# Input projection in seven-product form on x cast by DMA, residual added by DMA, MLP weights cast and summed in every group

## The chip, the cores and the metric

The kernel runs on all 8 cores of one Trainium2 chip. Each core works on its own 4096 tokens, and no core waits for another. The metric is device time in microseconds (us) of the slowest core, and less is better. Two kernels are compared on the same chip, in alternating rounds.

Each execution has a state. In the slow state the cores of one die, sometimes of both, show a lower granted TensorE clock than usual, and the execution takes some per cent longer. A ratio is the mean time of one kernel's fast runs over the mean time of the other kernel's fast runs of the same rounds, so it isn't quite the ratio of the medians that are quoted beside it.

PE is TensorE's matrix unit, PEld its weight loads, DVE VectorE, ACT ScalarE, POOL GpSimd and SP SyncE. The DMA share is the mean busy share of the core's 16 DMA engines.

## The reference

One block of a streaming encoder, width 1024, float32 in and out:

```python
h = rmsnorm(x, norm1_g)
b_gate, c_gate, xc, u, v = split(h @ w_in)        # 1024 -> 5 x 512
y_a = b_gate * causal_conv3(c_gate * xc, conv_w)
y_b = u * spatial_gating(layernorm(v), gmlp_ws, gmlp_bs)
y = concat(rmsnorm(y_a), rmsnorm(y_b))
x = x + y @ w_out                                 # the residual of this study
h2 = rmsnorm(x, norm2_g)
a = relu(h2 @ w_up)                               # 1024 -> 4096
x = x + (a * a) @ w_down
return rmsnorm(x, final_g)
```

## The kernel before

A core first runs the mixing stage over 8 tiles of 512 tokens, from about 20 to 400 us. Its result `x1` goes to HBM. Then the MLP runs over 4 groups of 1024 tokens; each group has two halves, and each half an up and a down projection. The 32 MLP weight blocks pass through a ring of six buffers, once per group, so 128 loads in all.

The output projection and the MLP are computed in a seven-product form: operands are split in 2x2 blocks, and seven block products replace eight. The price is sums: on each side the seven blocks come from four by four additions or subtractions, and the products are then added up. For the weights, `wsum` does the first part:

```python
def wsum(p, n):                       # three DVE instructions
    tt(p[:, 4], p[:, 3], p[:, 2], ALU.add, ...)
    tt(p[:, 3:6:2], p[:, 0:1] (twice), p[:, 3:5], ALU.subtract, ...)
    tt(p[:, 6], p[:, 1], p[:, 5], ALU.add, ...)
```

Before, these sums are formed once. 24 of the 32 weights are prepared during mixing and 8 at first use, and all seven blocks are stored in HBM as float16 (0.9 MB). The groups then load finished sums:

```python
def combine(p, dst, src, ...):
    dma("pool", p[:, 0:4], src[i % 16], ...)          # float32 -> float16, 1 MB read
    wsum(p, 128)
    dma("sp", dst, p[:, :], ...)                      # seven blocks to HBM

def load_w(n):
    if n < 32 and i >= 24:
        combine(RING[s], ws(i), wdn_d, ...)
    else:
        dma("sp", RING[s][:, :, :, :], ws(i), ...)    # 0.9 MB of float16
```

The input projection is plain, in matmuls of 512 columns. The residual is added by DVE straight from PSUM into the tile of x that is in SBUF anyway:

```python
def add(h, d_, bank):                 # in out_proj
    v = x[:, d_:d_ + 2, half * h:half * (h + 1)]
    tt(v, bank[:, :], v, ALU.add, ...)
# [cut] then dma("sp", x1_d part, x part)
```

## Time and profile before

| | before |
|---|---|
| time, median of 3 runs | 1234.01 us (1233.76 to 1235.53) |
| PE busy | 1195.1 us, 97% of the span |
| DVE, ACT busy | 76%, 43% |
| chain that ended last | 88% PE, 8% DMA |

From the page of the slowest core come the busy times, the PE and DMA rows of 40 slices (a digit is tenths of the slice that the unit was busy) and the chain of waits by engine:

```profile
PE 1195.1 (97%) x6264; PEld 584.4 (47%) x6264; DVE 939.3 (76%) x1460; ACT 533.5 (43%) x905; POOL 82.0 (7%) x144
...
PE   5899999999999999999999999999999999999994
...
DMA  7977888696676869357898954667964655975424
...
PE 88%; DMA 8%; DVE 1%; issue 1%; ACT 1%; SPq 0%; DVEq 0%; ACTq 0%; POOLq 0%
```

PE is the limit: it is busy for 90% or more of every slice but the first two and the last.

The windows view cuts one core's span into stretches. Its columns are the stretch, its length, then the busy time of PE, PEld, DVE, ACT and POOL (with the number of instructions), the granted clock, the DMA share and GB/s.

The timeline of PE shows small statistics products in each mixing tile (start, duration, instruction). The starts of the first one of each tile give the length of a tile:

```profile
175.99 0.59 PE L506 MATMUL PS<-SQ_61,ONESE 128*128 128x512 bf16 x2
227.57 0.59 PE L506 MATMUL PS<-SQ_61,ONESE 128*128 128x512 bf16 x2
277.42 0.59 PE L506 MATMUL PS<-SQ_61,ONESE 128*128 128x512 bf16 x2
327.69 0.59 PE L506 MATMUL PS<-SQ_61,ONESE 128*128 128x512 bf16 x2
```

Tiles are 50 to 52 us apart.

### The profile page before, as it was taken

What the parts mean: (1) busy time and instruction counts of PE and PEld (TensorE: products, weight loads), DVE (VectorE), ACT (ScalarE), POOL (GpSimd) and SP (SyncE); (2) the same over time, 40 slices, a digit from 0 to 9 for tenths busy, and PEclk for the clock granted to TensorE, in tenths of its full rate; (3) what the DMA queues carried; (4) which work ended last, traced back from release to release, by engine and by line L of the source; (5) the groups of instructions that cost most, each with busy time, mean ns of one, the idle gap of its engine ahead of it and who ended that gap; (6) DMA issues with size and microseconds to landing.
All of it is one profiled execution on the core that took longest, in us unless ns stands there. A gap on an engine that the chain in (4) does not pass through costs nothing.

```text
span 1233.4 us, 19511 instructions; the slowest of 8 cores (1226.8 to 1233.4 us)
## 1 busy us (share of the span) xinstructions
PE 1195.1 (97%) x6264; PEld 584.4 (47%) x6264; DVE 939.3 (76%) x1460; ACT 533.5 (43%) x905; POOL 82.0 (7%) x144
## 2 busy tenths in 40 slices
PE   5899999999999999999999999999999999999994
PEld 3345645546556464444444444444444444444442
DVE  2799889898899997448879747868746877856745
ACT  4554664555644555045047116217305417504533
POOL 0101011010001100001100100000000000100000
PEclk8999999999999999999999999999999999999998
DMA  7977888696676869357898954667964655975424
GB/s 184 163 162 197 202 219 202 175 258 153 176 234 182 294 219 301 119 183 174 222 309 270 282 204 159 212 199 223 296 230 150 218 185 172 296 252 179 150 90 137
DMA packets 60084, 253.87 MB, mean 206 GB/s; under 512 B 6224, under 2 KB 8400, under 8 KB 59984
## 3 DMA queue, kind: packets, MB, share of 16 engines
q1 hardware_dynamic: 38800, 182.36, 43.7%
q0 software_dynamic: 21184, 70.26, 25.9%
q8 instruction: 52, 0.85, 0.3%
q14 instruction: 48, 0.39, 0.1%
HBM read 211.71 MB, written 65.01 MB: 224 GB/s over the span
## 4 chain that ended last, share of the span: by engine, by line
PE 88%; DMA 8%; DVE 1%; issue 1%; ACT 1%; SPq 0%; DVEq 0%; ACTq 0%; POOLq 0%
PE PS L506 88%; DMA XS_92<-x_s 2%; DMA oT<-RA 1%; DMA RA<-x_s 1%; DMA WCXB_51<-wcxb 1%; DMA WV<-wv 1%; DMA X_75<-xT 1%; DMA WCXB_53<-wcxb 1%; DMA WSB_107<-wst 1%; DMA X_76<-xT 0%; DVE RB L522 0%; DVE RA L522 0%; SPq L533 0%; DVE H_93 L525 0%; ACT DUMP_57 L513 0%
## 5 line engine op out<-in xcount | busy, mean ns | idle before, releaser
L522 DVE TENSOR_TENSOR RB<-PS,RB 128x512 f32<-128x512 f32 x128 | 88.2, 690 | 84.6 <-PE PS L506 82.3
L522 DVE TENSOR_TENSOR RA<-PS,RA 128x512 f32<-128x512 f32 x96 | 66.0, 689 | 58.4 <-PE PS L506 55.6
L506 PE MATMUL PS<-YN,WO 128*128 128x256 f16 x896 | 104.7, 273 | 1.0 <-DVE YN L522 0.8
L522 DVE TENSOR_TENSOR A_86<-A_86 128x512 bf16<-128x512 bf16 (+1 forms) x192 | 93.9, 506 | 12.8 <-ACT A_86 L513 8.3
L506 PEld LDWEIGHTS PS<-YN,WO 128*128 128x128 f16 x896 | 87.3, 98 | 20.6 <-issue 2.8
L513 ACT ACTIVATE SN_88<-PS 128x512 f32<-128x512 f32 x63 | 37.2, 594 | 109.2 <-PE PS L506 108.7
L506 PE MATMUL PS<-A_86,RING_80 128*128 128x512 bf16 x308 | 76.7, 379 | 2.4 <-DVE RB L522 2.4
L506 PE MATMUL PS<-A_86,RING_82 128*128 128x512 bf16 x308 | 77.2, 379 | 0.0
L506 PE MATMUL PS<-A_86,RING_83 128*128 128x512 bf16 x308 | 77.1, 379 | 0.0
L506 PE MATMUL PS<-A_86,RING_81 128*128 128x512 bf16 x308 | 76.3, 379 | 0.0
L506 PE MATMUL PS<-H_93,RING_80 128*128 128x512 f16 x308 | 75.4, 379 | 0.0
L506 PE MATMUL PS<-H_93,RING_84 128*128 128x512 f16 x308 | 75.1, 379 | 0.0
L506 PE MATMUL PS<-H_93,RING_81 128*128 128x512 f16 x308 | 74.5, 379 | 0.0
L506 PE MATMUL PS<-H_93,RING_85 128*128 128x512 f16 x308 | 74.0, 379 | 0.0
L506 PE MATMUL PS<-A_86,RING_84 128*128 128x512 bf16 x280 | 69.6, 379 | 0.0
L513 ACT ACTIVATE SN_89<-PS 128x512 f32<-128x512 f32 x63 | 37.3, 594 | 74.5 <-PE PS L506 71.7
L506 PE MATMUL PS<-A_86,RING_85 128*128 128x512 bf16 x280 | 69.1, 379 | 0.0
L513 ACT ACTIVATE SN_87<-PS 128x512 f32<-128x512 f32 x66 | 39.0, 594 | 68.1 <-PE PS L506 64.7
L506 PE MATMUL PS<-H_93,RING_82 128*128 128x512 f16 x280 | 68.3, 379 | 0.0
L506 PE MATMUL PS<-H_93,RING_83 128*128 128x512 f16 x280 | 67.9, 379 | 0.0
L513 ACT ACTIVATE SN_90<-PS 128x512 f32<-128x512 f32 x64 | 38.1, 596 | 61.6 <-PE PS L506 61.3
L522 DVE TENSOR_TENSOR SN_89<-PS,SN_89 128x512 f32<-128x512 f32 x63 | 43.2, 688 | 24.8 <-PE PS L506 23.5
(237 smaller groups left out, 2078.4 us busy)
## 6 DMA issues: line engine op xcount, KB each, us to landing
RING_80<-ws_s SPq DMA_DIRECT2D x20, 896.0 KB, 5.9
RING_81<-ws_s SPq DMA_DIRECT2D x20, 896.0 KB, 6.3
RING_83<-ws_s SPq DMA_DIRECT2D x20, 896.0 KB, 6.5
RING_82<-ws_s SPq DMA_DIRECT2D x20, 896.0 KB, 5.6
RING_84<-ws_s SPq DMA_DIRECT2D x20, 896.0 KB, 6.2
RING_85<-ws_s SPq DMA_DIRECT2D x20, 896.0 KB, 6.2
ws_s<-PREP_70 SPq DMA_DIRECT2D x12, 896.0 KB, 5.7
ws_s<-PREP_69 SPq DMA_DIRECT2D x12, 896.0 KB, 6.0
```

The lines of the kernel that those rows point to most:

```text
L506: ins = e.matmul(real(o_), lhsT=l, rhs=r, start=st, stop=sp, skip_group_check=True)
L513: S.add("act", lambda e: e.activation(out=out, in_=real(in_), func=func, **kw), reads=reads, writes=writes, occ=(n / 1.2 + 100 + 70 * aps) ...
L522: dve(lambda e: e.tensor_tensor(out=out, in0=real(in0), in1=in1, op=op), reads, writes, n, rate, in0)
```

## The change

The intent is less PE work: the input projection gets the seven-product form too, which takes 280 matmuls of 256 columns per tile instead of 160 of 512. To pay for its sums and to make room in SBUF, DVE is relieved elsewhere. x arrives as float16, cast by the DMA, and isn't normalised. The residual is added by an accumulating DMA. The MLP's input isn't normalised either; its scale is carried to the residual and cancels in the last norm. The stored weight sums are gone: all 128 ring loads now read float32, cast, and form the sums again. The diffs here and below are shortened, with some helpers written out.

```diff
 def load_w(n):
-    if n < 32 and i >= 24:
-        combine(RING[s], ws(i), wdn_d, ...)
-    else:
-        dma("sp", RING[s][:, :, :, :], ws(i), ...)
+    dma("pool", p[:, 0:4, :, :], wup_d or wdn_d [i % 16], ...)   # 1 MB of float32, cast
+    wsum(p, 128)
 ...
 def load_x(m, chain=None, n=2):
-    dma("sp", X[...], xT part)                        # float32
+    dma("pool", HR[m % 2][:, j:j + n], xq[m, :, j:j + n], after, ...)   # cast to float16
 ...
 def out_proj(m):
-    winograd(prod, add, dc)                           # DVE adds PSUM to x
-    dma("sp", x1_d part, x part)
+    unit(prod, copy, copy, ...)                       # products into OB (copies on ACT, adds on DVE)
+    dma("pool", OB part, xT part, accum_op=ALU.add)   # residual
+    dma("sp", x1_d part, OB part)
 ...
-def stage_conv(m, c): ...   def stage_su(m, c): ...   def prep(i, n): ...
+def stage_c(m): unit(tprod(m, WC), ...)              # and stage_x, stage_v, gated alike
+def wsum_pe(w): ...                                   # first weight sums by identity matmuls
+def h_sums(m): ...                                    # sums of x's blocks, on DVE
```

## The prediction

> **What bounds the kernel now.** TensorE. On the page, PE is busy 1195.1 of 1233.4 us (97%), DVE 76%, ACT 43%; the chain of waits that ended last is 88% PE. From 150 us to the last down matmul at about 1217 the windows show PE busy almost throughout; the rest is start-up (about 20 us idle before 100 us, cold clock, DMA share about 1.0) and a 16 us tail. Only less PE work or a better start can pay, and a new wait can take it back.
>
> **PE.** In the timeline a 512-column matmul repeats every 216 ns and a 256-column one (64 of the output projection in 6.99 us) every 109 ns. The input projection has 160 of the former per token tile; in seven-product form 280 of the latter: 34.6 -> 30.6 us. Tile 0 stays plain, so 7 x 4.0 = 28 us go. Back come 66 identity matmuls forming weight sums at the start (14 us, partly in start-up holes) and some more statistics products. Summing both instruction orders with these durations: 1187 -> 1176 us. Net gain 11 us, not 28.
>
> **DVE and ACT.** Priced with durations of the trace (PSUM add 0.69 us, fp16 sum 0.42 for 512 and 0.68 for 1024 elements, f32 1024 product 1.22), DVE rises from 935 to about 1004 us: 96 more weight-sum triples (about 130 us) and the residual's products, against adds replaced by ACT's PSUM-to-PSUM copies, residual adds moved to DMA and dropped normalisations. ACT rises from 519 to about 700. In the mixing stage DVE falls to about 85% of a tile, ACT rises from 56% to over 80%. In the MLP, per half phase of 48.2 us PE, DVE carried 22 to 47 us; now 34 to 49. The fullest is the first down half of each group, 45 to 49: no slack.
>
> **DMA.** MLP weights now come as 1 MB of f32, cast, 128 times, not 0.9 MB fp16. From start-up and the queue table I estimate 4 us of all 16 engines per cast MB, against 2.7 for the old load: the MLP's DMA share goes from about 63% to about 85%. [...]its casts all sit on POOL's queue (25.9% of the engines' time). New coupling: DVE forms the sums in order, so a late weight stops DVE, and PE behind it.
>
> **On the critical path.** All PE time: -11. Start-up about -2 (loads still DMA-bound, but no x normalisation ahead of PE). New waits +5 to +20, mostly in the first up and down halves of groups 1 to 3, where output, residual loads and weights meet, and a little in mixing, where ACT copies gate the second product.
>
> **Predicted: 1224 us, 1209 to 1247 (8 in 10). Faster by over 2%: 0.10; within 2%: 0.83; slower: 0.07.**
>
> **What would show it.** Right: PE busy about 1180; mixing tiles about 47 us apart instead of 50; DVE over 90% in the first down halves, with small PE waits on DVE; DMA share over 0.8 through the MLP. Wrong: 256-column matmuls slower than 109 ns; PE idle of 30 us or more in the MLP behind weight loads (then slower); start-up idle under 10 us and PE without waits (then about 1205).
>
> **What would make it wrong.** Cast loads slower under load than at the start, so that six ring slots don't hide them; accumulating DMAs holding up output buffers; or a first tile beginning far earlier than the 18 us I expect.

"Its casts" are those of the trace of before: its DMA view has them on POOL's queue, with plain loads beside them. The windows of before, core 0, show what the start-up figures mean: a granted clock of 0.52 from 20 to 25 us and 0.80 from 25 to 30 us ("cold clock"), and a DMA share of 0.86 to 1.03 between 5 and 80 us, but for 0.62 from 20 to 25.

## More of the kernel before

The order of the instructions on each engine isn't written by hand. The program searches for it with a model of the engines and random draws, so any edit reshuffles all engines.

Core 0 of before, in mixing and at the entry of the MLP:

```profile
100.00:370.00 270.00, 269.19 (x1661) 148.71 (x1659) 246.02 (x349) 148.03 (x246) 22.85 (x43) 1.00 0.77 206
370.00:510.00 140.00, 139.83 (x797) 73.98 (x796) 119.82 (x178) 65.63 (x110) 12.63 (x21) 1.00 0.74 232
```

The length minus the first busy time is PE's idle time. It is 0.2 us at the entry, though that stretch holds the last tile of mixing, the first weights, the MLP's first inputs and the residual loads. The last number but one of each row, the DMA share, says that the DMA engines had a quarter of their time left.

The DMA view of the entry (kind of transfer, KB, median us from issue to landing) has the loads of the residual of the down projection, `RA` and `RB`:

```profile
RB<-x_s POOLq DMA_DIRECT2D x4, 512.0 KB, 12.9
RA<-x_s POOLq DMA_DIRECT2D x4, 512.0 KB, 11.9
```

## The result

The changed kernel is correct, and slower: 1285.39 us median (1271.72 to 1293.72, 4 runs, one of them slow) against 1234.77 us. The ratio of the fast runs is 1.0375 (95% interval 1.031 to 1.0441).

The same lines after. The page is that of core 7, the slowest:

```profile
PE 1214.1 (96%) x7346; PEld 699.0 (55%) x7346; DVE 997.9 (79%) x1654; ACT 697.8 (55%) x1203; POOL 115.9 (9%) x198
...
PE   4999999999997999999999989999999999989994
...
PEclk7999999999998788889999999999999999999997
...
DMA  9931663763459799456676965776896747897434
...
PE 84%; DMA 10%; DVE 2%; issue 2%; ACT 1%; SPq 0%; DVEq 0%; POOL 0%; ACTq 0%; POOLq 0%
```

The PE clock row dips from the thirteenth slice on. On cores 6 and 7 the granted clock was 0.81 from about 400 to 568 us. The other six cores, two of the same die among them, didn't hold it: from 510 to 568 us the windows view shows 1.00 on each of them. What set it off isn't shown. So the argument below uses core 0. The ratio above does contain this slower clock: cores 6 and 7 idled less (core 7 for 55.9 us in all, core 0 for 76.9) and were busy for longer (1214.1 us against 1192.6), and came out as late; and in each of the three fast runs some cores show a mean clock of 0.957 to 0.967, where the profiled run of before has 0.990 or more on every core. So core 0 is the measure of the waits, and the ratio is somewhat more than the waits alone. Its windows and its statistics products after:

```profile
100.00:370.00 270.00, 267.75 (x2569) 233.37 (x2568) 225.12 (x310) 205.97 (x371) 25.67 (x33) 1.00 0.50 106
370.00:510.00 140.00, 112.61 (x715) 68.11 (x714) 100.09 (x160) 81.48 (x140) 15.44 (x23) 0.94 0.92 193
...
1090.00:1150.00 60.00, 49.96 (x211) 21.28 (x209) 39.57 (x66) 6.01 (x10) 4.23 (x8) 0.91 0.80 163
```

```profile
130.35 0.59 PE L518 MATMUL PS<-SQ,ONESE 128*128 128x512 bf16 x2
175.78 0.59 PE L518 MATMUL PS<-SQ,ONESE 128*128 128x512 bf16 x2
221.20 0.59 PE L518 MATMUL PS<-SQ,ONESE 128*128 128x512 bf16 x2
268.38 0.59 PE L518 MATMUL PS<-SQ,ONESE 128*128 128x512 bf16 x2
```

Mixing did what it was meant to do: the tiles are 45 to 47 us apart, and PE idles for 2.2 of 270 us. The loss is in the next stretch. At the entry of the MLP PE idles for 27.4 us (140.00 - 112.61), and the DMA share is 0.92. Between 1090 and 1150 us another 10 us are lost.

A ledger for core 0, from the windows of both kernels. Its span grew by 36.1 us, from 1233.4 to 1269.5:

| PE idle time in (us) | before | after |
|---|---|---|
| 0 to 100 | 19.5 | 19.1 |
| 100 to 370 (mixing) | 0.8 | 2.2 |
| 370 to 510 (entry of the MLP) | 0.2 | 27.4 |
| 510 to 1090 | 2.4 | 3.2 |
| 1090 to 1200 | 0.0 | 10.0 |
| 1200 to the end | 15.5 | 15.0 |
| PE busy, whole span | 1195.1 | 1192.6 |

Idle time explains 38.6 us. The busy time fell by only 2.5 us, though the work fell by more, because matmuls ran slowly after the long pauses: in the first 3 us after a pause of 10.6 us, from 499.4 us on, the windows view shows a granted clock of 0.50, and from 502.4 us on 0.98 or more; after a pause of 5.9 us, from 1142 us on, it shows 0.50 for 3 us and 0.57 for 3 more. Core 0's mean clock was 0.983, where before had 0.992.

What stops PE there? The waits view of PE, core 0, 370 to 510 us (waited for: us in total, times, longest):

```profile
PE PS L518 <- DVE SN L539: 11.0, 2, 10.6
PE PS L518 <- ACT SN L525: 4.9, 2, 3.2
PE PS L518 <- ACT OB L525: 4.7, 3, 3.3
PE PS L518 <- ACT T L525: 4.4, 1, 4.4
```

They name DVE and ACT, but DVE was busy for only 100 of 140 us. The chain of waits of the same core, 370 to 530 us (start, us, what), names what those engines had waited for; its short pieces are left out:

```profile
378.57 19.41 DMA OB<-xT
398.05 9.37 DMA x_s<-OB
...
411.95 8.01 DMA OB<-xT
420.02 10.63 DMA x_s<-OB
...
444.86 17.47 DMA RING<-wup
...
469.10 25.35 DMA RB<-x_s
```

First the accumulating residual, then the store that must follow it, which holds the buffer OB; then a weight; then the residual of the down projection, for which DVE stood still for 11.4 us, with PE behind it for 10.6 us. The DMA view of that stretch, after (queue: packets, MB, share of the 16 engines; then each kind of transfer, as above):

```profile
q0 software_dynamic: 3493, 12.67, 55.8%
q1 hardware_dynamic: 4788, 14.18, 35.9%
...
OB<-xT POOLq DMA_DIRECT2D x9, 512.0 KB, 12.6
RING<-wup POOLq DMA_DIRECT2D x8, 512.0 KB, 17.4
...
RING<-wdn POOLq DMA_DIRECT2D x6, 512.0 KB, 13.8
RA<-x_s SPq DMA_DIRECT2D x4, 512.0 KB, 24.8
RB<-x_s SPq DMA_DIRECT2D x4, 512.0 KB, 25.6
```

Before, the loads of RA and RB took 11.9 and 12.9 us there. After, the median of all 64 RING<-wup on the page (core 7) is 6.3 us, and here it is 17.4. (The sizes are those of the destination; a cast from float32 to float16 reads twice as much.)

The 10 us lost after 1090 us are a wait of the same kind, and not for a weight. PE waited for DVE, which waited for the residual RB; the load of RB was issued only when stores of the output, one after another, had freed its buffer. The waits view of PE from 510 to 1200 us, and two pieces of the chain of waits:

```profile
PE PS L518 <- DVE RB L539: 13.2, 5, 5.9
...
1108.11 14.48 DMA oT<-RB
...
1122.65 17.32 DMA RB<-x_s
```

The theory (A): at the entry, late mixing and early MLP overlap, and the change gave both more DMA work, casting weight loads and accumulating residuals. Together they fill the DMA engines, the loads take two to three times as long, and those on PE's path stop PE. Rivals: (B) accumulation in itself, because a store, a reload and a free buffer wait behind it; (C) DVE, which forms 96 more weight sums and falls behind; (D) the order that the search happened to find.

### The profile page after: what moved, and what is told of

The parts are those of the page before. It is cut to its first block, busy times and chain, and to the rows that moved or that the text cites. A ratio compares the mean times of both kernels' runs of the same rounds, so it can differ in the third digit from the quotient of the medians.

```text
span 1270.0 us, 22374 instructions; the slowest of 8 cores (1255.6 to 1270.0 us)
## 1 busy us (share of the span) xinstructions
PE 1214.1 (96%) x7346; PEld 699.0 (55%) x7346; DVE 997.9 (79%) x1654; ACT 697.8 (55%) x1203; POOL 115.9 (9%) x198
## 4 chain that ended last, share of the span: by engine, by line
PE 84%; DMA 10%; DVE 2%; issue 2%; ACT 1%; SPq 0%; DVEq 0%; POOL 0%; ACTq 0%; POOLq 0%
PE PS L518 84%; DMA oT<-RB 3%; DMA x_s<-OB 2%; DMA OB<-xT 2%; DMA oT<-RA 1%; DMA RA<-x_s 1%; DMA RB<-x_s 1%; DMA WIN<-win 1%; DMA HR<-xq 1%; DVE RB L539 0%; DVE RA L539 0%; ACT RSY L525 0%; DVE A L539 0%; DVE RING L539 0%; ACT FSQ L525 0%
## 5 line engine op out<-in xcount | busy, mean ns | idle before, releaser
L518 PE MATMUL PS<-A,RING 128*128 128x512 bf16 x1792 | 408.7, 387 | 7.8 <-DVE RB L539 7.8
L518 PE MATMUL PS<-H,RING 128*128 128x512 f16 x1792 | 410.2, 388 | 0.0
L518 PEld LDWEIGHTS PS<-A,RING 128*128 128x128 f16 x1792 | 177.7, 99 | 229.4 <-issue 46.4
L518 PEld LDWEIGHTS PS<-H,RING 128*128 128x128 f16 x1792 | 178.6, 100 | 220.3 <-issue 40.6
L525 ACT ACTIVATE SN<-PS 128x512 f32<-128x512 f32 x256 | 149.7, 593 | 107.2 <-PE PS L518 101.8
L539 DVE TENSOR_TENSOR RING<-RING 128x512 f16<-128x512 f16 (+1 forms) x384 | 190.9, 505 | 6.0 <-DVE RING L539 0.5
L518 PE MATMUL PS<-HR,WIN 128*128 128x256 f16 x928 | 116.1, 277 | 2.2 <-ACT T L525 1.4
L518 PE MATMUL PS<-HD,WIN 128*128 128x256 f16 x896 | 112.4, 274 | 4.9 <-ACT T L525 3.4
L518 PEld LDWEIGHTS PS<-HR,WIN 128*128 128x128 f16 x928 | 91.4, 99 | 16.8 <-issue 3.0
L539 DVE TENSOR_TENSOR A<-A 128x512 bf16<-128x512 bf16 (+1 forms) x192 | 93.4, 506 | 5.2 <-ACT A L525 3.4
```

Source lines behind the costliest of these rows:

```text
L518: ins = e.matmul(real(o_), lhsT=l, rhs=r, start=st, stop=sp, skip_group_check=True)
L525: S.add("act", lambda e: e.activation(out=real(out), in_=real(in_), func=func, **kw), reads=reads, writes=writes, occ=(n / 1.2 + 100 + 70 ...
L539: dve(lambda e: e.tensor_tensor(out=out, in0=real(in0), in1=in1, op=op), reads, writes, n, rate, in0)
```

## The experiments

The expectations are quoted as they were written before each run; where they name theories by letter, each quotation says what its letters stand for.

Idle time below is the window's length minus PE's busy time, as a range over the eight cores; "later" is 510 to 1200 us. The unmodified change has 16.8 to 19.2 us at the start, 22.5 to 27.8 at the entry (cores 0 to 5) and 9.5 to 13.2 later (same cores).

| run | ratio to before (95%) | idle in mixing | idle at entry | DMA share, mixing / entry, core 0 |
|---|---|---|---|---|
| change | 1.0375 (1.031 to 1.0441) | 2 to 3 | 22 to 28 | 0.50 / 0.92 |
| e1_noacc | none given | 0 on core 0 | 5 to 7 | 0.26 / 0.74 |
| e5_plain | 1.0162 (1.0118 to 1.0205) | 2 to 3 | 12 to 18 | 0.42 / 0.88 |
| e2_resid (cores 0 to 3) | 1.0167 (1.0116 to 1.0218) | 3 on core 0 | 8 to 11 | 0.42 / 0.82 |
| e7_resid_gated | 1.015 (1.0111 to 1.0189) | 2 | 9 to 15 | 0.44 / 0.82 |
| b1_sums | 1.0079 (1.0044 to 1.0114) | 0 on core 0 | 0 to 2 | 0.30 / 0.72 |
| v2_cast (cores 0 to 3) | 1.0205 (1.0157 to 1.0252) | 19 to 38 | 3 to 13 | 0.97 / 0.81 |
| v4_half | 1.004 (1.0022 to 1.0057) | 2 to 3 | 8 to 9 | 0.64 / 0.65 |
| v5_more | 0.9934 (0.9912 to 0.9955) | 2 to 3 | 6 to 9 | 0.80 / 0.60 |
| v6_acc | 0.9959 (0.9894 to 1.0024) | 2 | 7 to 11 | 0.89 / 0.79 |

### Without the accumulating DMAs, and as plain copies

e1_noacc leaves the residual out, and its result is wrong. e5_plain keeps the transfers, but as plain copies that overwrite, also wrong.

```diff
-dma("pool", rows, part(xT), ..., accum_op=ALU.add)    # e1_noacc: gone
-dma("pool", rows, part(xT), ..., accum_op=ALU.add)    # e5_plain
+dma("pool", rows, part(xT), ...)
```

> The changed kernel without its 32 accumulating DMAs (x1 is then the output projection alone: a wrong result on purpose). Theory A (the residual by accumulating DMA fills the DMA engines where the mixing stage meets the MLP, 375 to 505 us; the nine of that stretch cost about 2.9 us of all 16 engines each): PE idle in the entry to the MLP falls from 27 us to under 10, the time to about 1240 or less. Rival B (the cast weights and the reloads of x1 saturate it anyway): PE idle there stays over 18 us, time over 1260. Theory C (the 0.81 clock stretch is set off by PE pausing and resuming): goes with the idle, mean clocks back to 0.985 or more on all cores; rival D (it comes from the denser mixing stage): the 0.81 stretch stays on some core in most runs.

> The same 32 DMAs on the same queue, but plain copies that overwrite the tile (wrong on purpose). If the accumulation itself is what costs (2.9 us of the engines against 1.4 for a plain one of that size), half or more of what e1 gains is gained here: about 1250. If it is the extra step in the chain (copy, DMA, store) and its place in the queue, little is gained: 1265 to 1285.

Without them, two fast runs took 1248.43 and 1238.07 us, and two were slow; the fast runs of before in the same rounds were 1232.83 to 1239.3 us. That is a ratio of 1.006, worked out from the means of 1243.3 and 1235.9, on few runs. Plain copies took 1256.76 us. The entry's idle time fell from 22 to 28 us to 12 to 18 (plain) and 5 to 7 (none). So the residual's DMA is worth most of the loss in this setting, and part of that is there for a plain copy too: it is the traffic and the chain of transfers, not the addition alone. (Later idle time didn't go in e1_noacc: it was 0 to 19 us by core. Its theories C and D, of the clock, stay open: its two fast runs have mean clocks of 0.982 or more on every core.)

The prices can be read in mixing (100 to 370 us), where nothing is short (DMA shares of 0.26 to 0.50). The DMA view of core 0 gives POOL's queue 12.2% of the 16 engines without the residual transfers (10 casts of x; one weight was issued, but hardly begun), 29.7% with 23 plain ones issued besides and 37.5% with 23 accumulating ones. The ten casts were 1440 packets, so a transfer of 512 KB is 144 packets, and the packets of the window (4712 and 4571) say that 22.7 plain and 21.7 accumulating ones were moved in it. So an x cast costs 3.3 us of all 16 engines, a plain transfer 2.1 and an accumulating one 3.1. (The expectations had 1.4 and 2.9. The 1.4 fits SP's queue in the change from 150 to 350 us, 13.3% of 200 us for 19 plain transfers; the 2.9 is an estimate from the same stretch.) At the entry of the change, POOL's queue moved 3493 packets, or 24.3 transfers, in 78 us (55.8% of 140): 10.3 accumulations, which are the 32 less the 21.7, and 14 casting weight loads. At 3.1 us an accumulation, a weight cost 3.3 us. Later, without accumulations, 31 of them took 52.4% of 190 us (510 to 700 us), 3.2 us each.

### The residual on VectorE

e2_resid loads the residual into OB ahead of the products, with a plain DMA on SP's queue, and lets DVE add the products. e7_resid_gated also makes the first of those loads wait for the last weight of the start, because e2_resid idled for 21 to 25 us at the start instead of 17 to 19.

```diff
+for i, j, rows, part in parts:
+    dma("sp", rows, part(xT), [], ...)             # e7: gate[-1] if m == 0 else []
 prod(bA, P1, True, False)
 fork(bA, bD)
 prod(bD, P2, False, True)
-copy(q11, bD)                                      # ACT
+plus(q11, bD)                                      # DVE, onto the residual; the others alike
 ...
-    dma("pool", rows, part(xT), ..., accum_op=ALU.add)
```

> The residual as before: x loaded by a plain DMA before the output projection and added by VectorE from PSUM, six adds per unit instead of four ACT copies and two adds (correct result). Theory A: the entry to the MLP loses most of its 27 us of PE idle, time about 1245; VectorE goes from 42 to about 47 of each 50 us in mixing, which may cost a few us there. Rival B: over 1260.

> The run before it with the residual by VectorE loaded x for the first output projection at the very start, among the weights, and PE's start-up idle rose from about 18 to 23 us. Here that first load waits for the last weight of the output projection (correct result). Expected: start-up idle back to 17 to 19, entry to the MLP as there (8 to 10 us of idle), time about 1248 to 1252. If it stays at 1258, the 4 us at the start were not what the slowest core was missing.

Both are correct, at 1258.33 and 1256.49 us. Over half of the loss is gone, and the rest stays (theory A had expected about 1245, then 1248 to 1252): in e7_resid_gated the entry still idles for 9 to 15 us at a DMA share of 0.82, and single cores lose up to 7.5 us between 700 and 760 us. Rival B alone doesn't suffice.

### The casting weight loads alone, in the kernel before

b1_sums is the kernel before, with nothing changed but the weights: no preparation in mixing, 128 casting loads, sums in every group.

```diff
-    if n < 32 and i >= 24: combine(...)
-    else: dma("sp", RING[s], ws(i), ...)
+    dma("pool", p[:, 0:4], wup_d or wdn_d [i % 16], ...)
+    wsum(p, 128)
```

> The kernel before with only this part of the change: weights cast from f32 and summed in every group, nothing stored (correct result). My prediction gave the MLP 5 to 20 us of new waits from this part; if the cast loads are the cause of the loss at the MLP's entry (rival B), this kernel shows DMA share near 1.0 and PE idle of 15 us or more there and lands at 1250 or more. Theory A: 1230 to 1243, waits under 10 us.

It took 1245.43 us, 0.8% more. DVE and its order carry all the added sums here, and the entry is fine (0 to 2 us idle). The later idle time is 1 to 12 us by core. On core 2 the waits view of PE, 510 to 1220 us, names the weights themselves:

```profile
PE PS L506 <- DMA RING<-wdn: 4.9, 2, 4.6
PE PS L506 <- DVE RB L522: 1.7, 1, 1.7
```

On core 5 the longest waits there are for DVE's sums onto RB (3.9 us in 3 waits). So casting loads with their sums went with some 10 us more, a difference no larger than what another order can make (below). It is the pause at the entry that is missing here: it takes the casting loads and the residual's traffic together to make it.

### Casting the weights once

If theory A holds, the cure is fewer bytes at the entry. v2_cast keeps the change as it is (with accumulation) and casts each of the 32 weights once, HBM to HBM, during mixing, six per tile. The ring then loads half a megabyte of float16 and DVE still forms every sum. v1_both does this on top of e7_resid_gated, and v3_x0 is v1_both with one wait less at the start (the one of e4_x0, below).

```diff
+dma("pool", w16_d[i], (wup_d or wdn_d)[i % 16], [("yn", m)], ...)   # six per tile
 ...
-dma("pool", p[:, 0:4], (wup_d or wdn_d)[i % 16], ...)
+dma("pool", p[:, 0:4], w16_d[i], ...)
```

> The changed kernel with one thing different: while the mixing stage has DMA to spare (share 0.5), each MLP weight is cast once from f32 in HBM to fp16 in HBM, and the ring loads 0.5 MB of fp16 in every group; VectorE forms the sums in every group as in the change, and the residual stays an accumulating DMA (correct result). Theory A2 (the MLP's new waits are DMA waits: 1 MB casts fill the DMA engines): DMA share of the MLP falls from about 0.75 to about 0.5, PE idle from 760 us on to under 4 us, at the entry from 27 to 12 or less, time about 1225 to 1235. Rival E (VectorE, at over 90% with the sums, is what makes PE wait): the idle after 510 us stays at 8 us or more on the slowest core, time over 1245.

> Both: residual by VectorE from a gated plain load, and weights cast once during mixing. Theory A with A2: entry idle under 5 us, later idle under 4, so what is left is the start and the tail; PE work is 11 us less than in the kernel before: 1216 to 1226, a little faster than before. Rival E: over 1240, VectorE waits named in the waits of PE.

> As v1, and the fourth piece of the first x tile is not held until the first has landed. In the changed kernel PE waited until 21.3 us for statistics of x whose last piece was issued at 8.6 us and landed at about 16. Expected: PE's first projection 2 to 4 us earlier, time 2 to 3 us less than v1; if the loads are limited by the engines' rate alone, nothing.

v2_cast took 1263.9 us, v1_both 1329.09 (ratio 1.0743) and v3_x0 1283.68 (1.0382). All three missed their expectations: they lost in mixing what they gained later. In v1_both a store of 512 KB, issued at 138 us on SP's queue behind casts on POOL's, took 63.6 us to land, while the windows view shows a DMA share of 1.00 until 185 us. PE idled for 64 to 82 us in mixing. In v3_x0 it was 46 to 52 us, 45 us less in all for one wait at the start, where 2 to 3 us were expected; why isn't shown. From 138 to 185 us POOL's queue took 88.7% of the 16 engines and SP's 10.2%: a queue of its own didn't spare the store the wait.

But v2_cast settled rival C for the later waits. Two rows of its windows, core 0:

```profile
510.00:700.00 190.00, 187.27 (x858) 84.75 (x869) 154.37 (x274) 93.52 (x154) 16.36 (x31) 1.00 0.43 138
700.00:1150.00 450.00, 448.31 (x2055) 203.96 (x2086) 383.23 (x671) 203.66 (x336) 38.52 (x73) 1.00 0.48 152
```

DVE does all its sums and is as busy as in the change, yet PE idles for at most 2.7 us in either stretch: with the DMA share down from about 0.7 to 0.45, the waits after 510 us are gone. They were waits for DMA.

### Fewer casts, paced

v4_half builds on e7_resid_gated and casts 16 weights, three per tile, each released by a different step of the tile; each cast is written as 128 rows of a padded buffer, where v1_both's had been merged into 16 long ones. v5_more casts 24, four per tile. In both the first x tile's fourth piece isn't held back.

```diff
-dma("pool", w16_d[i], ..., [("yn", m)], ...)                 # six at one step
+dma("pool", w16_d[i, :, 0:2048], ..., [("tick", t % 3, m)], ...)
```

> The version with the residual added by VectorE (e7_resid_gated), with the fourth piece of the first x tile not held back behind the others, and with 16 of the 32 MLP weights (those of the first half of each group) cast once to float16 in HBM during the mixing stage, three per tile, each after a different step of the tile, and written as 128 rows rather than as 16 long ones; the ring then loads those 16 in float16, half a megabyte each, in every group. The other 16 are cast on loading, as in the change. Theory A (the entry of the MLP stalls because the DMA engines are saturated there, and the later waits are late casting loads): the DMA share between 370 and 510 us falls from about 0.82 to about 0.6, PE's idle time there falls from 9 to 14 us to under 5 us per core, and the sum of the later idle stretches falls from 4 to 20 us to under 5; mixing keeps under 5 us of idle time because the casts are spread, with a DMA share of about 0.65 to 0.75; the time is 1228 to 1240 us, about level with the kernel before. Rival B (the entry stalls for a reason other than the amount of data, such as the order of the loads or buffers coming free late): the entry's idle time stays at 9 to 14 us and the time is 1245 to 1257 us. If casts in HBM delay the small transfers of mixing whatever their pacing, as they did when six went in a row, mixing shows 15 us or more of idle time and the time is over 1250 us.

> The same as v4_half, but with 24 of the 32 MLP weights cast in HBM during mixing, four per tile, so that only the eight down-projection weights of each group's second half are still cast on loading. Theory A (what remains of the later waits of v4_half, 1 to 15 us by core, is casting loads that land late): the DMA share of mixing rises from 0.65 to about 0.72 without pauses of PE, the later idle stretches fall to under 3 us on every core, the entry keeps its 8 us because VectorE and ScalarE hold PE there and not the DMA engines, and the time is 1229 to 1237 us, level with the kernel before or a little under it. Rival B (the later waits come from VectorE's sums or from buffers): the later idle stretches stay at up to 10 us, and the time is 1237 to 1243 us, or more if the added casts delay mixing.

v4_half took 1241.11 us, 0.4% above the kernel before. Its idle time, 8 to 9 us at the entry and 3 to 10 later, was more than the 5 us expected. v5_more took 1231.16 us against 1237.99: 0.9934, with an interval that excludes 1. It is correct, and the fastest version tried, though by less than 1%. Its windows on core 0, to be held against those of before and of the change:

```profile
100.00:370.00 270.00, 267.05 (x2537) 232.71 (x2545) 250.75 (x358) 183.20 (x329) 17.88 (x34) 1.00 0.80 163
370.00:510.00 140.00, 132.64 (x811) 76.88 (x816) 133.46 (x212) 69.61 (x117) 9.53 (x18) 1.00 0.60 184
...
1090.00:1150.00 60.00, 59.52 (x274) 26.69 (x275) 47.81 (x86) 28.26 (x49) 5.81 (x11) 1.00 0.44 107
```

Its DMA view at the entry:

```profile
q1 hardware_dynamic: 5734, 16.18, 37.8%
q0 software_dynamic: 2592, 9.44, 21.9%
...
RING<-w_s POOLq DMA_DIRECT2D x18, 512.0 KB, 5.4
...
RA<-x_s SPq DMA_DIRECT2D x5, 512.0 KB, 7.0
RB<-x_s SPq DMA_DIRECT2D x5, 512.0 KB, 5.5
```

A weight now costs 1.7 us of the 16 engines (21.9% of 140 us, over 18) instead of 3.3, and lands in 5.4 us instead of 17.4; the residuals land in 5.5 to 7 us instead of 25. The DMA work moved to mixing, where there was room: the share there went from 0.50 to 0.80 with 2 to 3 us of idle time, as in the change. What remains at the entry, 7 us, doesn't look like DMA any more: DVE is busy for 133 of 140 us, and PE's waits there are for DVE and ACT, none of them over 1.5 us (core 0). Nor is POOL's queue slow in itself while DVE works: these weights come by it and land in 5.4 us, with DVE busy for 133 us of the 140, where the change has 100.

Between v1_both and v4_half the casts' number, pacing and shape changed (and the start's gate, as in v3_x0). In mixing the casts landed in a median of 28 to 30 us in v1_both (core 0) and 6.2 to 6.4 in v4_half (core 3), the stores in 5.8 and 4.6. Which of the three mattered isn't separated.

### Accumulation with the casts paced

v6_acc is v5_more with the accumulating DMAs of the change in place of VectorE's adds; from the change it differs in the casts and in the start's gate.

> The change itself, with its accumulating DMA transfers kept, plus the 24 paced casts in HBM of v5_more and the fourth piece of the first x tile not held back. Against v5_more it differs only in how the residual is added. Theory A (the accumulating transfer costs twice the DMA time of a plain one, and a store and a reload wait behind it, so it is a cost of its own at the entry of the MLP and, with DMA engines that are now fuller, in mixing): DMA share of mixing about 0.9, PE's idle time there 5 to 30 us; entry idle time 10 to 20 us against 6 to 8 in v5_more; under 3 us later; time 1240 to 1265 us. Rival B (only the casting loads were too much, the accumulation itself costs nothing once they are gone): entry and mixing idle as in v5_more, time 1226 to 1235 us.

Four fast runs took 1226.1 to 1242.63 us, ratio 0.9959 (0.9894 to 1.0024). The expectation of theory A, 1240 us or more, missed: I had taken accumulation for a cost of its own (its "twice" is the 2.9 against 1.4 us of e5_plain's expectation; in mixing it was 3.1 against 2.1). With the weights out of the way it costs hardly anything that these runs can resolve. Mixing holds a DMA share of 0.89 with 2 us of idle time, and the entry idles for 7 to 11 us against 6 to 9. So neither part of the change is to blame alone. Each fits while the sum fits; together, they don't. It also settles rival C at the entry: DVE forms every sum there as in the change, and the entry's idle time is 7 to 11 us instead of 22 to 28.

### The start

e4_x0 is the change with one wait taken away: the fourth piece of the first x tile isn't issued after the first has landed, but at once.

```diff
-after = [] if chain is None else chain[-3]
+after = [] if chain is None or m == 0 else chain[-3]
```

> The change with one wait taken away at the start: the fourth piece of the first x tile is issued with the other three instead of after the first of them has landed. If that wait ate the start-up gain that the prediction counted on, PE's longest wait for the sum of squares at the start falls from 15.5 us to about 11 us and its idle time over the first 100 us falls by 1 to 4 us; if the weights' loads are what counts there, it stays at 17 to 19 us. The rest is as in the change, so the time is 1265 to 1290 us and shows nothing of it.

The longest wait of PE at the start, for the squares of x, on core 0; first the change, then e4_x0:

```profile
PE PS L518 <- DVE XQ L539: 15.5, 1, 15.5
```

```profile
PE PS L518 <- DVE XQ L539: 10.9, 1, 10.9
```

The start's idle time fell from 16.8 to 19.2 us to 13.4 to 16.5 us. A hand-written gate ate the gain that the prediction had counted on. But the whole time was 1263.49 us, ratio 1.0207 where the change has 1.0375, and some 6 us of that difference lay at the entry (16 to 21 us idle instead of 22 to 28), which the edit doesn't touch. (The clock differed too: 0.975 or more on every core of its fast runs.) That raised rival D.

### Another order of the same program

The change with seeds 2 and 3 of the search instead of 1, and v5_more with seed 2; nothing else differs.

```diff
-rnd = random.Random(1)
+rnd = random.Random(2)
```

> The change itself, the order's search started from another seed (2 instead of 1), nothing else. If the loss comes from the amount of DMA work at the entry of the MLP, this order shows it too: DMA share 0.88 or more between 370 and 510 us, PE idle there 15 to 28 us per core, 5 to 15 us of later idle time, time 1260 to 1290 us. If it was the luck of the first order, the time is 1225 to 1250 us. The spread between the seeds says how far two versions must differ before a difference means anything.

> The change itself with seed 3, as c1_seed2: 1260 to 1290 us if the loss is systematic, with 15 to 28 us of idle time of PE at the MLP's entry; 1225 to 1250 us if the first order was bad luck.

> v5_more (residual added by VectorE, 24 weights cast in HBM during mixing) with seed 2. If its lead over the kernel before comes from the DMA engines having room, another order keeps it within about 8 us: 1225 to 1240 us, entry idle 5 to 12 us, later idle under 3 us. If v5_more was a lucky order, 1240 us or more.

These three ran on a chip where every run, those of before too, had mean granted clocks of 0.93 to 0.97, and before took 1291.11 us. The medians were 1299.02, 1292.84 and 1289.44 us. Some of these runs count as fast, probably because there is no faster one of the same kernel to compare with, so their ratios (1.0063 and 0.9998 for the two seeds of the change) aren't used. The change idled there for only 7 to 14 us at the entry, at a DMA share of about 0.9, where 15 to 28 were expected: this fits a slower PE that asks for its data later, but isn't shown. The same programs again, on another chip:

> The program of c1_seed2 again, unchanged, in hope of a chip in the fast state (kernel before near 1236 us). If the loss is systematic: 1260 to 1290 us, PE idle for 15 to 28 us between 370 and 510 us at a DMA share of 0.88 or more. If it was the first order's bad luck: 1225 to 1250 us.

> The program of c2_seed3 again, unchanged: 1260 to 1290 us with 15 to 28 us of idle time at the MLP's entry if the loss is systematic, 1225 to 1250 us if not.

> The program of c3_v5seed again, unchanged: 1225 to 1240 us, entry idle 5 to 12 us and later idle under 3 us if v5_more's lead is not the luck of its order; 1240 us or more if it is.

| run | median us | ratio (95%) | idle at entry | DMA share at entry |
|---|---|---|---|---|
| c1b_seed2 (change) | 1273.67 | 1.0296 (1.023 to 1.0362) | 18 to 23 | 0.92 to 0.96 |
| c2b_seed3 (change) | 1279.05 | 1.0311 (1.0256 to 1.0366) | 18 to 23 | 0.90 to 0.93 |
| c3b_v5seed (v5_more) | 1235.68 | 0.9979 (0.9939 to 1.0019) | 7 to 10 | 0.61 to 0.67 |

The loss is systematic: three orders lose 3.0 to 3.75%, all at a saturated entry. The size isn't exact: with e4_x0, four orders of practically the same program range from 1.0207 to 1.0375. So one order more or less, with the clock that it met, is worth up to 1.7% when DMA is short (some 3 us, or 0.2%, of that are e4_x0's shorter start), and differences such as that between e2_resid and e5_plain mean nothing. For v5_more the two orders are 0.9934 and 0.9979: level with the kernel before or slightly faster, and no more than that is shown.

## Why the prediction was wrong

It said 1224 us (1209 to 1247), and gave a slowdown of over 2% a chance of 0.07. The result is 1285 us.

- **PE work, -11 us: right.** In v5_more, where pauses don't blur it, PE's busy time averages 1183.2 us over the cores with a full set of records, against 1194.6 before: -11.4. A 256-column matmul did repeat every 109 ns, and the mixing tiles are 45 to 47 us apart (predicted about 47). In the change itself pauses hid the gain: core 0 was busy for 1192.6 us, as matmuls ran at a granted clock of 0.50 for 3 us and more after its pauses of 5.9 and 10.6 us.
- **Start-up, -2 us: didn't come.** Idle time stayed at 19 us on core 0. The gate on x's fourth piece was the cause (e4_x0).
- **New waits, +5 to +20, "mostly in the first up and down halves of groups 1 to 3": this step failed, in size and in place.** They were 39 us more on core 0, and 27 of them lay at the entry of group 0, which the prediction didn't look at. There the last tile's residuals, six ring loads, the MLP's inputs and the residual loads fall together. The prediction averaged DMA over the MLP and never summed it for that stretch. The sum, as the traces give it afterwards: in 140 us, 14 casting loads at 3.2 us (the later MLP's price), 10.3 accumulations at 3.1 (mixing's) and 50 us of SP's queue (35.9%) are 127 us, a share of 0.91 (measured: 0.92), and the loads there took two to three times as long. The 10 us that did come later weren't waits for weights either: they were for a residual load behind stores of the output.
- **"The MLP's DMA share goes from about 63% to about 85%": too high on average, too low where it mattered.** Core 0 shows 0.70, 0.80, 0.72 and 0.80 in the four stretches from 510 to 1150 us, against 0.77, 0.57, 0.69 and 0.56 before. The price of a cast, 4 us in the prediction, was 3.2 to 3.3, so the price isn't what failed.
- **DVE and ACT sums: right.** DVE was 998 us (predicted 1004), ACT 698 (about 700). That the first down half of each group would have "no slack" didn't decide anything: v2_cast keeps DVE's work and has no waits after 510 us.
- **"A late weight stops DVE, and PE behind it": right as a mechanism.** DVE waited 5.2 us for a weight and 11.4 us for a residual at the entry, and PE stood behind it.
- **What would make it wrong** named cast loads slower under load and accumulating DMAs holding output buffers. Both came true, at the same place. That they would add up was the thought that was missing, and the chance of 0.07 was too small for a risk that was written down.

Shown by runs: relieving the entry of either load brings most of PE's time back (e1_noacc, v4_half, v5_more, v6_acc), DVE's sums alone don't cost it (v6_acc), the later waits are DMA waits (v2_cast), and the loss holds for three orders. Not shown: how 27 us divide between accumulation and casts, since the two aren't additive; what set off the clock of 0.81, and its part of the ratio; and what of v1_both's failure was the number, the pacing or the shape of its casts.

## What to carry to other kernels

Sum the DMA engines' time stage by stage, in prices read from the trace (here, for 512 KB at the destination, of all 16 engines: 2.1 us plain on POOL's queue, 1.4 on SP's, 3.1 us accumulating, 3.2 to 3.3 us cast from float32, 1.7 us for a float16 weight), above all where one stage's end overlaps the next one's start: here mixing ran with 2 us of pauses at a share of 0.89 (v6_acc), but the entry, whose transfers stand in PE's path one after the other, lost 9 to 15 us at 0.82 (e7_resid_gated) and 22 to 28 at 0.92, where its loads took two to three times as long. At the entry the loads of RA and RB took 5.5 to 7 us at a share of 0.60 (v5_more), 12 to 13 at 0.74 (before, by POOL's queue), 9 to 14 at 0.79 (v6_acc) and 25 at 0.92 (the change), all on core 0, so the share alone doesn't give the time of a load. Moving work from DVE to DMA, and forming sums again instead of storing them, was free only where that sum had room (v6_acc), and the mend was to move bytes to a stage that had it, in small portions (v5_more). When a search orders the program, run another seed of it before believing a difference of one or two per cent: four orders of practically the same program lay up to 1.7% apart here.
